# A pooling mixer whose last 32 tokens use a quarter of TensorE's columns, with the norm moved into the pooling matrices

## The chip, the cores and the metric

The kernel runs on one core of one Trainium2 chip. TensorE multiplies matrices and writes to eight banks of PSUM; VectorE (DVE) and ScalarE (ACT) do elementwise work and read those banks; GpSimd (POOL) does a few elementwise operations on SBUF; SyncE (SP) issues nearly all DMAs. The metric is the time of one execution in microseconds of device time. Three runs of the kernel before took 953.94, 954.66 and 955.35 us; their median is 954.66 us.

## What is computed

A decoder of two layers on 256 tokens with 16 meta tokens ahead of them (272 in all), 1024 features wide, in float32. Each layer is a feed-forward network, a mixer and a second feed-forward network, each with an RMS norm before and after it and a residual. The mixer of the first layer averages over the last 2, 4, 8 or 16 tokens, by group of 256 features, and then multiplies each group by its own matrix:

```python
def rmsnorm(x, g):
    y = xf * lax.rsqrt(jnp.mean(xf * xf, axis=-1, keepdims=True) + EPS)
    return (y * g.astype(jnp.float32)).astype(x.dtype)

def causal_multiscale_pool(h, w, b, scale):
    ...
    for g, win in enumerate(POOL_WINDOWS):          # 2, 4, 8, 16
        lo = jnp.maximum(t + 1 - win, 0)
        cnt = (t + 1 - lo).astype(jnp.float32)
        pooled.append((csg[:, 1:, g] - csg[:, lo, g]) / cnt[None, :, None])
    diff = (pooled - hg).astype(h.dtype)
    y = jnp.einsum('blgc,gcd->blgd', diff, w) + b
    return y.reshape(bsz, L, D) * scale

# in the first layer
    f = swiglu(rmsnorm(h, ffn_norm_pre[i, 0]), ...)
    h = h + 0.5 * rmsnorm(f, ffn_norm_post[i, 0])
    hn = rmsnorm(h, mix_norm_pre[i])
    m = causal_multiscale_pool(hn, pool_w[j], pool_b[j], pool_scale[j])
    h = h + rmsnorm(m, mix_norm_post[i])
```

The norm is a factor for each token, the pooling a matrix between tokens, and the group's weights a matrix between features, so the kernel takes them in another order: weights first, then the norm's factor, then the pooling.

## The kernel before

The hidden state `h` lies transposed in SBUF: eight tiles of 128 features by 272 tokens, the 256 tokens first and the 16 meta tokens behind them. Most of the time goes to the products with the weights of the feed-forward networks and of the attention, which TensorE makes in three products for each weight tile (high by high, low by high, high by low). This change touches none of them. It touches `pool_mix`, the mixer of the first layer, which stands between the first feed-forward network (`ffn(0, ...)`) and the second (`ffn(1, ...)`).

The engines PE, ACT, DVE and SP run in the order in which the code is written; what a tile must wait for is worked out from who reads and writes its buffer. A tile with a tag that an earlier tile had takes over that tile's buffer, and its first write waits for the last reader of the earlier one. Two such tags matter here. The mixer's eight weight tiles `wps` (`wp` in the profile) have the tags `xlo0` to `xlo7`; and `Post.old(j)`, which puts `h[j]` times the gain of the next norm into the tile `a` for the next network (line 430), has the tag `xlo{j}` too.

`pool_mix` goes through these steps; lines are those of the profile.

- Twelve products of constants keep TensorE at work while VectorE is alone (line 269, `WARM0`).
- VectorE finishes the post-norm of the network before and adds it onto `h` (lines 701 to 709), tile 0 and tile 1 alone and then two tiles at a time. ScalarE squares `h` two tiles at a time into `psq` (711).
- TensorE makes the inner products with `wps` (690): for each of the eight tiles of `h` one product of 256 columns for each of three blocks of 128 tokens, which are 0 to 127, 128 to 255 and 144 to 271. The third block serves the 16 meta tokens and the 16 tokens at the end. The results `z` fill six banks.
- VectorE adds the squares to `pacc2` (715 to 718) and TensorE sums them over the features, one column for each block (720). These three products stand ahead of the inner products of tiles 6 and 7 (`LATE`).
- ScalarE and VectorE make the reciprocal root (281, 275 to 277) and copy `z` to SBUF times the norm's factor of each token, `zs` (729 to 734).
- For each of the eight output tiles three products with the pooling matrices `bands` (742, 743, 746), whose columns are 128 + 144 + 32; behind each ScalarE squares the result (453), VectorE adds up the squares (464), and for the tiles in `EARLY` VectorE also writes `bt`, the result times its gain (446).
- A few more constant products (`WARM2`), then the tail: `b` of tiles 1 and 2 (435), `bt` of the tiles in `BESIDE`, the sum of squares over the features in two products (470, 471), its reciprocal root `ny` (281), and for the first three tiles of the next network `x = a + b * ny` (312, 314), with which TensorE starts the second network (522).

The lines that set the buffers and the waits in question:

```python
wps.append(act.tile([P, 256], F32, tag=f"xlo{q}", name="wp"))
a = act.tile([P, L], F32, tag=f"xlo{j}", name="a")
```

Of the kernel before, what the change touches and what calls it, by code (L numbers as in the profile page):

```python
# [9 lines left out]
F32 = mybir.dt.float32  # L10
F32R = mybir.dt.float32r
AF = mybir.ActivationFunctionType
ALU = mybir.AluOpType
# [3 lines left out]
P = 128  # L17
D = 1024
NK = D // P
NMETA = 16  # L20
SEQ = 256
L = NMETA + SEQ
# [33 lines left out]
POOL_SQ = ((0, 2), (2, 4), (4, 6), (6, 8))  # L56
# [12 lines left out]


C_FPRE, C_FPOST, C_MPRE, C_MPOST, C_PB, C_PS, C_SUB, C_META = 0, 32, 64, 80, 96, 104, 112, 113
# [108 lines left out]
def trunk(ctx, tc, ht, w13a, w13b, w2t, w2n, wqkva, wqkv, wo, wp, lamv, mask, band, gpost, out):  # L180
    nc = tc.nc
# [5 lines left out]
    tmp = ctx.enter_context(tc.tile_pool(name="tmp", bufs=2))  # L187
# [4 lines left out]
    bands = early.enter_context(tc.tile_pool(name="bands", bufs=1, side="right")).tile([P, 4, 176], F32, name="bands")  # L192
    wps = []
# [53 lines left out]
    pbs = const.tile([P, NK], F32, name="pbs")  # L247
# [152 lines left out]
    class Post:  # L400
# [273 lines left out]
    def pool_mix(old, ps, post):  # L674

        def bank():
            return ps.tile([P, 512], F32, tag="bank", name="bank")


        tok = ((0, P), (P, 2 * P), (L - P, L))  # L680

        z = [[bank() for _ in tok] for _ in range(2)]
        sums = bank()[:, 0:3]
        idle = bank()
        warm(lambda: idle, ones, WARM0, P)

        def inner(j):
            g = j // 2
            for ti, (t0, t1) in enumerate(tok):
                nc.tensor.matmul(z[g // 2][ti][:, (g % 2) * 256:(g % 2 + 1) * 256],  # L690
                                 lhsT=h[j][:, t0:t1], rhs=wps[j], start=j % 2 == 0, stop=j % 2 == 1)

        with tc.tile_pool(name="poolw", bufs=1, reuse_waits="tile") as pw:
            sq = pw.tile([P, NK, L], F32, name="psq")
            zs = [pw.tile([P, D], F32, name=f"zs{ti}", tag=f"zs{ti}") for ti in range(3)]
            ys = []


            old.begin_refine()
            t = tmp.tile([P, L], F32, tag="rt", name="rt")  # L700
            nc.vector.tensor_tensor(t, btall[:, 0], old.y, ALU.mult)
            old.slope()
            nc.vector.scalar_tensor_tensor(t, old.c, 1.5, t, ALU.add, ALU.mult)
            nc.vector.tensor_tensor(h[0], h[0], t, ALU.add)
            old.finish()
            for lo, hi in POOL_H[1:]:
                t = pw.tile([P, 3, L], F32, tag="pt", name="pt", bufs=2)[:, :hi - lo]
                nc.vector.tensor_tensor(t, btall[:, lo:hi], old.r.unsqueeze(1).to_broadcast([P, hi - lo, L]), ALU.mult)
                nc.vector.tensor_tensor(hall[:, lo:hi], hall[:, lo:hi], t, ALU.add)
            for lo, hi in POOL_SQ:  # L710
                nc.scalar.activation(out=sq[:, lo:hi], in_=hall[:, lo:hi], func=AF.Square)
            for j in range(NK - LATE):
                inner(j)
            acc = pw.tile([P, 2, L], F32, name="pacc2")
# [3 lines left out]
            nc.vector.tensor_tensor(acc[:, 0], acc[:, 0], acc[:, 1], ALU.add)  # L718
            for ti, (t0, t1) in enumerate(tok):
                nc.tensor.matmul(sums[:, ti:ti + 1], lhsT=acc[:, 0, t0:t1], rhs=ones[:, 0:1], start=True, stop=True)  # L720
            for j in range(NK - LATE, NK):
                inner(j)
            for j in range(post.ahead):
                post.old(j)
            r2 = rsqrt(sums, 3, True, "rc", 3)

            def normed(q):
                at = slice(q * 512, (q + 1) * 512)
                nc.scalar.mul(out=zs[0][:, at], in_=z[q][0], mul=r2[:, 0:1])
                nc.vector.tensor_scalar(zs[1][:, at], z[q][1], r2[:, 1:2], None, ALU.mult)  # L730
                if q:
                    nc.vector.tensor_scalar(zs[2][:, at], z[q][2], r2[:, 2:3], None, ALU.mult)
                else:
                    nc.scalar.mul(out=zs[2][:, at], in_=z[q][2], mul=r2[:, 2:3])

            def pooled(j):

                y = bank()
                ys.append(y)
                g = j // 2  # L740
                c = slice(j * P, (j + 1) * P)
                nc.tensor.matmul(y[:, P:SEQ], lhsT=zs[1][:, c], rhs=bands[:, g, 0:P], start=True, stop=True)
                nc.tensor.matmul(y[:, 0:P + NMETA], lhsT=zs[0][:, c], rhs=bands[:, g, 0:P + NMETA],
                                 start=False, stop=True, skip_group_check=True)
                ends = y.rearrange("p (a b) -> p a b", b=SEQ)[:, :, 0:NMETA]
                nc.tensor.matmul(ends, lhsT=zs[2][:, c],
                                 rhs=bands[:, g, P + NMETA:].rearrange("p (a b) -> p a b", b=NMETA),
                                 start=False, stop=True, skip_group_check=True)
                post.squared(j, y[:, :L], vt[:, C_PS + j:C_PS + j + 1], pbs[:, j:j + 1], add=False)
                if j:  # L750
# [8 lines left out]
            normed(0)  # L759
            normed(1)  # L760
            for j in range(NK):
                pooled(j)
                if j == 0:
                    first(0)
                if j in EARLY:
                    scaled(j, True)
            s = bank()
            warm(lambda: s, ones, WARM2, P)
            for j in range(1, post.ahead):
                first(j)  # L770
            for j in BESIDE:
                scaled(j, True)
            post.rms(lambda: s, True)
            for j in range(NK):
                if j not in EARLY + BESIDE:
                    scaled(j)
# [395 lines left out]
    with tc.tile_pool(name="ps", bufs=8, space=PSUM) as ps:  # L1172
        warm(lambda: ps.tile([P, 512], F32, tag="bank", name="bank"), ones, WARM_START, P)
        post = Post(L, half[:, 0:8], C_MPRE, AHEAD[0])
# [7 lines left out]
        old, post = post, Post(L, psg, C_FPRE + 8, AHEAD[1])  # L1182
# [36 lines left out]
def _layout(x, meta_tokens, ffn_norm_pre, ffn_norm_post, ffn_w1, ffn_w3, ffn_w2, mix_norm_pre, mix_norm_post,  # L1219
# [42 lines left out]
    t = np.arange(2 * NMETA)  # L1262
    d = np.concatenate([t[NMETA:], t[:NMETA]])[None, None, :] - t[:NMETA, None, None]
    count = np.minimum(np.concatenate([t[NMETA:], t[:NMETA]]) + 1, win)
    ends = np.zeros((P, 4, 2 * NMETA))
    ends[P - NMETA:] = np.where((d >= 0) & (d < win), 1.0 / count, 0.0) - (d == 0)
# [23 lines left out]
```

## Time and profile before

| | before |
|---|---|
| runs | 953.94, 954.66, 955.35 us |
| profiled execution, its time | 954.47 us |
| its span, first to last instruction | 952.7 us |
| mean granted clock of TensorE | 0.998 |
| TensorE's longest gap inside the span | 1.69 us, ahead of 230.54 |

The span is the time from the first to the last instruction of one profiled execution; some 1.8 us of its time lie around it. In the profile PE is TensorE's products, PEld its weight loads. A row of a timeline gives start and duration in us, engine, line, operation, tile written, tiles read, shapes and a count, and in brackets the idle time ahead of it with what ended that. Rows that follow each other with the same line and tiles are merged into one.

### The profile page before, as it was taken

The page shows a single profiled execution, that of the slowest core. Times are in us where ns is not written, and L with a number is a line of the kernel's source. Part 1 is how long each engine was busy: PE and PEld are TensorE (multiplying, and loading weights), DVE is VectorE, ACT ScalarE, POOL GpSimd, SP SyncE. Part 2 cuts the span into 40 slices and gives each one's busy share as a digit, 9 for nine tenths or more (in the row PEclk, how much of TensorE's full clock was granted, in tenths as well). Part 3 has the DMA queues.
Part 4 walks back from the last instruction along what each step waited for, and adds up shares of the span by engine and source line. Part 5 has one row for each costly group of instructions (what it writes and reads, how often), then busy time and mean ns, then how long its engine had stood idle before and what let it go on. Part 6 is the DMA issues. An engine that isn't in the chain of part 4 may idle for free.

```text
span 952.7 us, 17430 instructions
## 1 busy us (share of the span) xinstructions
PE 940.8 (99%) x6937; PEld 904.5 (95%) x6937; DVE 637.2 (67%) x1094; ACT 501.9 (53%) x863; POOL 14.7 (2%) x22
## 2 busy tenths in 40 slices
PE   9999999999999999999999999999999999999997
PEld 9999999998999999999999999999998998888885
DVE  7955554458975555448955554468876899767774
ACT  7744444435654445545744455446776756445442
POOL 0000000210000000000000000000001000000000
PEclk9999999999999999999999999999999999999999
DMA  9755557630375556551755556532523628655521
GB/s 337 239 204 177 166 155 222 219 119 2 116 267 174 175 159 192 179 195 42 257 194 177 163 167 187 187 106 90 177 89 120 212 90 287 223 188 180 185 89 44
DMA packets 48320, 160.74 MB, mean 169 GB/s; under 512 B 5360, under 2 KB 8944, under 8 KB 48240
## 3 DMA queue, kind: packets, MB, share of 16 engines
q1 hardware_dynamic: 47952, 159.31, 52.2%
q8 instruction: 54, 0.88, 0.4%
q10 hardware_dynamic: 288, 0.33, 0.1%
q14 instruction: 26, 0.21, 0.1%
HBM read 158.57 MB, written 1.05 MB: 168 GB/s over the span
## 4 chain that ended last, share of the span: by engine, by line
PE 94%; DVE 3%; ACT 1%; issue 1%; DMA 0%; DVEq 0%; ACTq 0%
PE bank L257 23%; PE bank L256 23%; PE bank L255 23%; PE bank L522 8%; PE bank L1120 7%; PE bank L1122 4%; DVE wlo L149 1%; PE bank L643 1%; PE bank L655 1%; PE bank L644 1%; DMA raw<-in_w13a 0%; ACT sc L844 0%; PE bank L821 0%; PE bank L812 0%; PE bank L811 0%
## 5 line engine op out<-in xcount | busy, mean ns | idle before, releaser
L149 DVE TENSOR_TENSOR wlo<-raw,whi 128x1024 fp32r<-128x1024 f32 (+1 forms) x296 | 353.5, 1197 | 58.9 <-PE bank L256 28.4
L137 ACT CAST whi<-raw 128x1024 fp32r<-128x1024 f32 (+1 forms) x296 | 299.8, 1029 | 51.4 <-PE bank L257 45.9
L255 PE MATMUL bank<-x,whi 128*128 128x272 f32 (+1 forms) x752 | 217.3, 289 | 0.0
L257 PE MATMUL bank<-x,whi 128*128 128x272 f32 (+1 forms) x752 | 216.8, 288 | 0.0
L256 PE MATMUL bank<-x,wlo 128*128 128x272 f32 (+1 forms) x752 | 215.7, 287 | 0.2 <-DVE wlo L149 0.2
L256 PEld LDWEIGHTS bank<-x,wlo 128*128 128x128 f32 x752 | 141.3, 188 | 0.5 <-DVE wlo L149 0.4
L255 PEld LDWEIGHTS bank<-x,whi 128*128 128x128 f32 x752 | 141.3, 188 | 0.5 <-issue 0.4
L257 PEld LDWEIGHTS bank<-x,whi 128*128 128x128 f32 x752 | 141.6, 188 | 0.0
L256 PE MATMUL bank<-ghi,wlo 128*128 128x272 f32 x484 | 140.0, 289 | 0.0
L255 PE MATMUL bank<-ghi,whi 128*128 128x272 f32 x484 | 140.0, 289 | 0.0
L257 PE MATMUL bank<-glo,whi 128*128 128x272 f32 x484 | 140.0, 289 | 0.0
L573 ACT ACTIVATE ua<-ua 128x272 f32<-128x272 f32 (+1 forms) x88 | 37.1, 429 | 143.0 <-DVE ua L559 143.0
L582 ACT CAST ghi<-ua 128x272 fp32r<-128x272 f32 (+1 forms) x88 | 36.1, 417 | 111.7 <-DVE ua L579 111.7
L255 PEld LDWEIGHTS bank<-ghi,whi 128*128 128x128 f32 x484 | 91.8, 190 | 0.0
L257 PEld LDWEIGHTS bank<-glo,whi 128*128 128x128 f32 x484 | 91.2, 188 | 0.0
L256 PEld LDWEIGHTS bank<-ghi,wlo 128*128 128x128 f32 x484 | 90.9, 188 | 0.0
L257 PE MATMUL bank<-xlo,whi 128*128 128x272 f32 x304 | 87.8, 289 | 0.0
L255 PE MATMUL bank<-xhi,whi 128*128 128x272 f32 x304 | 87.4, 287 | 0.0
L256 PE MATMUL bank<-xhi,wlo 128*128 128x272 f32 x304 | 87.3, 287 | 0.0
L579 DVE TENSOR_TENSOR ua<-bank,ua 128x272 f32<-128x272 f32 (+1 forms) x69 | 29.5, 437 | 71.1 <-PE bank L257 71.1
L1120 PE MATMUL bank<-xp,whi 128*128 128x512 f32 x304 | 76.1, 392 | 0.0
L1120 PEld LDWEIGHTS bank<-xp,whi 128*128 128x128 f32 x304 | 55.5, 188 | 10.5
(232 smaller groups left out, 1376.8 us busy)
## 6 DMA issues: line engine op xcount, KB each, us to landing
raw<-in_w13b SPq DMA_DIRECT2D x152, 512.0 KB, 4.1
raw<-in_w2t SPq DMA_DIRECT2D x48, 448.0 KB, 3.4
raw<-in_w2t SPq DMA_DIRECT2D x24, 512.0 KB, 3.5
raw<-in_w2n SPq DMA_DIRECT2D x22, 512.0 KB, 3.8
raw<-in_w13a SPq DMA_DIRECT2D x18, 512.0 KB, 4.2
raw<-in_wqkv SPq DMA_DIRECT2D x18, 512.0 KB, 4.3
raw<-in_wo SPq DMA_DIRECT2D x8, 512.0 KB, 3.7
raw<-in_wqkva SPq DMA_DIRECT2D x6, 512.0 KB, 4.2
```

Of the source, the lines that this page charges most:

```text
L137: self.nc.scalar.copy(out=hi[:, :n], in_=self.raws[u][:, :n])
L149: self.nc.vector.tensor_tensor(lo[:, :n], raw[:, :n], hi[:, :n].bitcast(F32), ALU.subtract)
L255: nc.tensor.matmul(out_ap, lhsT=a[0], rhs=b[0], start=start, stop=False)
L256: nc.tensor.matmul(out_ap, lhsT=a[1], rhs=b[0], start=False, stop=False)
L257: nc.tensor.matmul(out_ap, lhsT=a[0], rhs=b[1], start=False, stop=stop)
L522: nc.tensor.matmul(us[q][:, :n], lhsT=taken[u][a][:, c * P:(c + 1) * P], rhs=x[:, :n], start=start, stop=stop)
L573: nc.scalar.activation(out=a[:, :self.n], in_=a[:, :self.n], func=AF.Silu)
L579: nc.vector.tensor_tensor(s[:, :n], self.sum(u3), s[:, :n], ALU.mult)
L582: nc.scalar.copy(out=hi, in_=s[:, :n])
L643: nc.tensor.matmul(y[:, :n], lhsT=a[0], rhs=x[0], start=b == 0, stop=False)
L1120: nc.tensor.matmul(u, lhsT=parts[0][:, k * P:(k + 1) * P], rhs=res.pairs[k], start=k == 0, stop=k == NK - 1)
L1122: nc.tensor.matmul(u[:, :n], lhsT=parts[1][:, k * P:(k + 1) * P], rhs=res.x[k][0], start=False, stop=k == NK - 1, skip_group_check=True)
```

## The change

Inside `pool_mix`:

- The third token block is gone from the inner products. The last 32 tokens (the 16 at the end and the 16 meta tokens) get products of their own behind the sums, `inner_ends`: 32 tokens wide, so each result takes 32 rows of one bank `ze`. The two tiles of a feature group share 32 rows, and the four groups lie under each other, each on its own quarter of TensorE's columns. Their sums of squares become four products of 32 rows.
- All inner products of the two whole blocks stand ahead of the sums.
- `z` is copied to SBUF without the norm's factor, three of four copies on ScalarE and one on VectorE. The factor goes into the pooling matrices instead: `sb` is `bands` with each row times the factor of its token, made by VectorE, ScalarE and GpSimd, for the first group alone and then for the other three.
- `Post.old` of tiles 0 and 1 stands on ScalarE between the squares of `h` and the copies; tile 2 follows behind `zse`.
- VectorE adds the post-norm onto `h` two tiles at a time from the start, and makes the products of tiles 4 to 7 ahead of their sums.
- The first two output tiles are multiplied before the first product with the ends. Tile 4 goes from `EARLY` to `BESIDE`, so its `bt` is made in the tail.
- The squares of the last output tile but one are no longer added by VectorE: `Post.rms` takes them as a third product.
- `WARM0` goes from 12 to 14 and `WARM2` from 3 to 1. On the host, `band` holds the matrices of the ends at the rows of each group.

```diff
-LATE = 2
-POOL_H = ((0, 1), (1, 2), (2, 4), (4, 6), (6, 8))
-WARM0 = 12
-WARM2 = 3
-EARLY = (0, 3, 4)
-BESIDE = (1, 2, 5)
+WARM0 = 14
+WARM2 = 1
+EARLY = (0, 3)
+BESIDE = (4, 1, 2, 5)
...
-        def rms(self, bank, eps, refill=0):
+        def rms(self, bank, eps, refill=0, apart=1):
...
-            nc.tensor.matmul(s[:, :n], lhsT=ones, rhs=self.sq[NK - 1][:, :n], start=False, stop=True)
+            for j in range(NK - apart, NK):
+                nc.tensor.matmul(s[:, :n], lhsT=ones, rhs=self.sq[j][:, :n], start=False, stop=j == NK - 1)
...
-        tok = ((0, P), (P, 2 * P), (L - P, L))
+        tok = ((0, P), (P, 2 * P))
         z = [[bank() for _ in tok] for _ in range(2)]
+        ze = bank()
...
+        def inner_ends():
+            for j in (0, 2, 4, 6, 1, 3, 5, 7):
+                g = slice(j // 2 * 32, j // 2 * 32 + 32)
+                nc.tensor.matmul(ze[g, 0:256], lhsT=h[j][:, L - 32:L], rhs=wps[j], start=j % 2 == 0, stop=j % 2 == 1)
...
+            product(2)
+            total(2)
+            product(4)
+            product(6)
+            total(4)
+            total(6)
...
-            for j in range(NK - LATE):
+            for j in range(NK):
                 inner(j)
+            for j in range(2):
+                post.old(j)
+
+            nc.scalar.copy(out=zs[0][:, 0:512], in_=z[0][0])
+            nc.scalar.copy(out=zs[1][:, 0:512], in_=z[0][1])
...
+            for g in range(4):
+                nc.tensor.matmul(sums[g * 32:g * 32 + 32, 2:3], lhsT=acc[:, 0, L - 32:L], rhs=ones[:, 0:1],
+                                 start=True, stop=True)
+            inner_ends()
+            nc.scalar.copy(out=zs[0][:, 512:1024], in_=z[1][0])
+            nc.vector.tensor_copy(zs[1][:, 512:1024], z[1][1])
+            r2 = rsqrt(sums, 3, True, "rc", 3)
...
+            nc.vector.tensor_scalar(sb[:, 0, 176:], bands[:, 0, 0:P], r2[:, 1:2], None, ALU.mult)
+            nc.scalar.mul(out=sb[:, 0, 0:P + NMETA], in_=bands[:, 0, 0:P + NMETA], mul=r2[:, 0:1])
+            nc.gpsimd.tensor_scalar(sb[:, 0, P + NMETA:176], bands[:, 0, P + NMETA:], r2[:, 2:3], None, ALU.mult)
+            nc.scalar.copy(out=zse, in_=ze[:, 0:256])
+            for j in range(2, post.ahead):
+                post.old(j)
+            nc.vector.tensor_scalar(sb[:, rest, 176:], bands[:, rest, 0:P], r2[:, 1:2], None, ALU.mult)
+            nc.vector.tensor_scalar(sb[:, rest, 0:P + NMETA], bands[:, rest, 0:P + NMETA], r2[:, 0:1], None, ALU.mult)
+            nc.gpsimd.tensor_scalar(sb[:, rest, P + NMETA:176], bands[:, rest, P + NMETA:], r2[:, 2:3], None, ALU.mult)
...
-            post.rms(lambda: s, True)
+            post.rms(lambda: s, True, apart=2)
```

What stands in the queues at two places. On TensorE, from the inner products to the second output tile, before (the numbers behind `pacc` and `zs` are those of buffers):

```order
L690 MATMUL bank<-wp,h 128x256 x18
L720 MATMUL bank<-ones,pacc_2635 128x1 x3
L690 MATMUL bank<-wp,h 128x256 x6
L742 MATMUL bank<-bands,zs_2590 128x128
L743 MATMUL bank<-bands,zs_2589 128x144
L746 MATMUL bank<-bands,zs_2591 128x2x16
```

The same place in the changed program, whose line numbers differ:

```order
L688 MATMUL bank<-wp,h 128x256 x16
L740 MATMUL bank<-ones,pacc_2601 128x1 x2
L742 MATMUL bank<-ones,pacc_2601 32x1 x4
L694 MATMUL bank<-wp,h 32x256 x8
L767 MATMUL bank<-sb,zs_2591 128x128
L768 MATMUL bank<-sb,zs_2590 128x144
L767 MATMUL bank<-sb,zs_2591 128x128
L768 MATMUL bank<-sb,zs_2590 128x144
L773 MATMUL bank<-sb,zse 128x2x16 x2
```

The last readers of `wp` 0 to 7 moved behind the sums. On ScalarE, from the squares of `h` to the first square of an output tile, with the engines or DMA queues whose semaphores a row waits for; before:

```order
L711 ACTIVATE psq<-h 128x544 [waits DVE_49] x4
L430 ACTIVATE a<-h 128x272 [waits PE_49,Pool_49] x3
L281 ACTIVATE ny<-bank,eps_c 128x3 [waits PE_49]
L729 ACTIVATE zs_2589<-bank,ny 128x512 [waits DVE_49]
L734 ACTIVATE zs_2591<-bank,ny 128x512
L729 ACTIVATE zs_2589<-bank,ny 128x512 [waits PE_49]
L453 ACTIVATE sq<-bank,pbs,h 128x272 [waits PE_49]
```

And in the changed program:

```order
L727 ACTIVATE psq<-h 128x544 [waits DVE_49] x4
L426 ACTIVATE a<-h 128x272 [waits PE_49,Pool_49] x2
L733 COPY zs_2590<-bank 128x512
L734 COPY zs_2591<-bank 128x512
L745 COPY zs_2590<-bank 128x512
L277 ACTIVATE ny<-bank,eps_c 128x3
L752 ACTIVATE sb<-bands,ny 128x144 [waits DVE_49]
L754 COPY zse<-bank 128x256 [waits PE_49]
L426 ACTIVATE a<-h 128x272 [waits Pool_49]
L449 ACTIVATE sq<-bank,pbs,h 128x272 [waits PE_49]
```

Three copies came in between `a` and `ny`, and neither they nor `ny` wait for TensorE themselves any more.

More of the change, by code (lines that the diff above doesn't have):

```diff
@@ L705, in pool_mix @@
+            nc.vector.tensor_tensor(hall[:, 0:2], hall[:, 0:2], t, ALU.add)
             old.finish()
[L706 to L711, printed above, removed]
@@ L712, in pool_mix, with product, total @@
-            for j in range(NK - LATE):
+            acc = pw.tile([P, 2, L], F32, name="pacc2")
+            more = {}
+            def product(lo):
+                more[lo] = pw.tile([P, 2, L], F32, tag="pt", name="pt", bufs=3)
+                nc.vector.tensor_tensor(more[lo], btall[:, lo:lo + 2], old.r.unsqueeze(1).to_broadcast(each), ALU.mult)
+            def total(lo):
+                nc.vector.tensor_tensor(hall[:, lo:lo + 2], hall[:, lo:lo + 2], more[lo], ALU.add)
+            product(2)
@@ L713, in pool_mix @@
+            total(2)
[3 more added lines that the diff above has]
+            total(6)
+            for lo in (0, 2, 4, 6):
+                nc.scalar.activation(out=sq[:, lo:lo + 2], in_=hall[:, lo:lo + 2], func=AF.Square)
+            for j in range(NK):
                 inner(j)
-            acc = pw.tile([P, 2, L], F32, name="pacc2")
+            for j in range(2):
+                post.old(j)
+            nc.scalar.copy(out=zs[0][:, 0:512], in_=z[0][0])
+            nc.scalar.copy(out=zs[1][:, 0:512], in_=z[0][1])
@@ L720, in pool_mix @@
                 nc.tensor.matmul(sums[:, ti:ti + 1], lhsT=acc[:, 0, t0:t1], rhs=ones[:, 0:1], start=True, stop=True)
-            for j in range(NK - LATE, NK):
-                inner(j)
-            for j in range(post.ahead):
-                post.old(j)
[L725 to L734, printed above, removed]
+            for g in range(4):
[5 more added lines that the diff above has]
+            r2 = rsqrt(sums, 3, True, "rc", 3)
+            zse = pw.tile([P, 256], F32, name="zse")
+            sb = pw.tile([P, 4, 176 + P], F32, name="sb")
+            rest = slice(1, 4)
+            nc.vector.tensor_scalar(sb[:, 0, 176:], bands[:, 0, 0:P], r2[:, 1:2], None, ALU.mult)
[3 more added lines that the diff above has]
+            for j in range(2, post.ahead):
+                post.old(j)
+            nc.vector.tensor_scalar(sb[:, rest, 176:], bands[:, rest, 0:P], r2[:, 1:2], None, ALU.mult)
+            nc.vector.tensor_scalar(sb[:, rest, 0:P + NMETA], bands[:, rest, 0:P + NMETA], r2[:, 0:1], None, ALU.mult)
+            nc.gpsimd.tensor_scalar(sb[:, rest, P + NMETA:176], bands[:, rest, P + NMETA:], r2[:, 2:3], None, ALU.mult)
             def pooled(j):
@@ L1264, in _layout @@
     count = np.minimum(np.concatenate([t[NMETA:], t[:NMETA]]) + 1, win)
+    each = np.where((d >= 0) & (d < win), 1.0 / count, 0.0) - (d == 0)
     ends = np.zeros((P, 4, 2 * NMETA))
-    ends[P - NMETA:] = np.where((d >= 0) & (d < win), 1.0 / count, 0.0) - (d == 0)
+    for g in range(4):
+        ends[g * 32 + NMETA:g * 32 + 32, g] = each[:, g]
     r["band"] = c(np.concatenate([inside, ends], axis=2).astype(np.float32))
```

35 lines of the change are left out of this document (19 added, 16 removed).

## The prediction

> **What bounds the kernel now.** I read the page first, then the chain of work that ended last inside the pooling stage, then each engine's timeline there. The page says that TensorE is the bound almost everywhere:
>
> ```profile
> span 952.7 us, 17430 instructions
> PE 940.8 (99%) x6937; PEld 904.5 (95%) x6937; DVE 637.2 (67%) x1094; ACT 501.9 (53%) x863; POOL 14.7 (2%) x22
> ```
>
> The program's order outside the mixer is the same before and after on every engine, so only the mixer counts: it lies between the last product of the first feed-forward network (205.6 us) and the first product of the second (230.54 us). There TensorE isn't the bound throughout. The chain of waits (start, duration, engine, tile, line):
>
> ```profile
> 214.37 0.74 DVE h L709
> ...
> 217.43 0.45 DVE pacc L718
> 217.88 0.04 issue
> 217.92 0.83 PE bank L720 x6
> 218.75 2.70 PE bank L690 x12
> 221.45 0.22 PE bank L742 x2
> ...
> 226.99 0.58 ACT sq L453
> 227.56 0.48 ACT b L435
> 228.04 0.03 issue
> 228.07 1.50 DVE bt L446 x3
> 229.56 0.36 DVE rt L312
> 229.92 0.02 issue
> 229.95 0.45 DVE x L314
> 230.40 0.14 issue
> 230.54 3.53 PE bank L522 x26
> ```
>
> To see here: VectorE adds the post-norm onto `h` until 215.1 and sums the squares until 217.87. TensorE then takes the three sums, the last twelve passes of the inner products, and from 221.3 the eight pooled tiles. A tail on ScalarE and VectorE ends it. I follow one question through the change: when can the first pooled product start, which is at 221.29 now, and is the 9.25 us from there to 230.54 still the same?
>
> **The change, part by part.** *Wider steps on VectorE.* The timeline of VectorE gives the durations (start, duration, engine, line):
>
> ```profile
> 207.45 0.44 DVE L701 TENSOR_TENSOR rt<-bt,ny 128x272 f32<-128x272 f32 x1 [5.39 <-ACT ny L281]
> 208.14 0.44 DVE L505 SCALAR_TENSOR_TENSOR nt<-bank,nt 128x272 f32<-128x272 f32 x1 [0.25 <-ACT nt L502]
> 211.58 0.72 DVE L709 TENSOR_TENSOR h<-h,pt 128x544 f32<-128x544 f32 x1
> ```
>
> One tile takes 0.44, two take 0.72; a step that needs the one before starts 0.03 after its end, another 0.08 before it. The five one-tile steps for tiles 0 and 1 become three two-tile steps (2.2 to 2.16 us), and with the products of 4 to 7 put ahead of their sums most steps no longer need the one just before them. Laid out one after another, the starts are 207.45, 208.14, 208.62, 209.38, 210.02 and 210.56, then 211.31, 211.95, 212.59, 213.22 and 213.87: `h` is whole at 214.6 instead of 215.1, and the sum of squares at 217.4 instead of 217.87. The first tile comes 0.56 later (210.1), and two more warming products cover that. **Gain 0.5 us so far.**
>
> *Inner products.* The timeline of TensorE:
>
> ```profile
> 217.92 0.83 PE L720 MATMUL bank<-ones,pacc 128*128 128x1 f32 x6
> 218.61 2.84 PE L690 MATMUL bank<-wp,h 128*128 128x256 f32 x12
> ```
>
> A product is two passes (x12 for the order's x6), and a pass of 256 columns takes 2.84 less its last drain of 0.38 over 11, 0.22 us. The 32 passes that stay end with 16 passes that start when `h` 4 and 5 are there (213.95 plus 0.1): 217.5. The sums follow without a wait: four full passes and eight narrow ones. The nearest row with a narrow pair is in the attention stage, where the last two of the six passes have 16 columns:
>
> ```profile
> 649.97 0.63 PE L921 MATMUL bank<-ones,acc 128*128 128x1 f32 x6
> ```
>
> It is no longer than six full ones (0.83), so I give all sums 0.9, and the products into quarter columns start at 218.4. Whether these run beside each other no row shows for columns. From both sides: one after another they take 16 passes of 0.22, 3.5 us; four at once 0.9 us. The nearest rows are products on halves of the array's rows in the attention stage:
>
> ```profile
> 657.33 0.52 PE L811 MATMUL bank<-kf,qf 64*128 64x144 f32 x4
> 657.68 0.63 PE L812 MATMUL bank<-kf,qf 64*128 64x272 f32 x4
> ```
>
> Four passes of 272 columns would need 0.92 at 0.23 each; they take 0.63 with the drain, so two stand beside two. I take 0.9 and keep 3.5. The Trainium skill, TensorEngine Tiling (Array Packing), section Key Properties, says that different tiles run their loads and products in parallel; by that rule it would be 0.9, and the row agrees for halves of the rows.
>
> *The two early `a` tiles on ScalarE.* This decides. `a` of tile 0 and tile 1 has the tag of the buffer that held the mixer's weights `wp` 0 and 1. Its write must wait for the last product that reads them. That was an early inner product; it is now a quarter-column product, behind the sums. The rows of order above show it: the three copies of `z` and the table's `ny` follow on ScalarE with no wait on TensorE of their own, so the wait in front of them covers the sums too. ScalarE takes its instructions in the program's order. Its timeline before:
>
> ```profile
> 215.13 0.66 ACT L711 ACTIVATE psq<-h 128x544 f32<-128x544 f32 x1 [0.74 <-DVE h L709]
> 215.69 1.33 ACT L430 ACTIVATE a<-h 128x272 f32<-128x272 f32 x3
> 218.79 0.26 ACT L281 ACTIVATE ny<-bank,eps_c 128x3 f32<-128x3 f32 x1 [1.76 <-PE bank L720]
> 219.74 0.69 ACT L729 ACTIVATE zs<-bank,ny 128x512 f32<-128x512 f32 x1 [0.69 <-DVE ny L277]
> ```
>
> Now: the last square ends at 215.3, and ScalarE stands still until the first quarter product has drained, at 219.0 (218.4 plus two passes and a drain of 0.16). `a` 0 starts at 219.1. The fifth quarter product, which frees `wp` 1, is done at 219.4 (side by side), `a` 1 at 219.5, 0.41 later (1.33 for three, each 0.51 long). Then three copies of 512 columns out of the bank; the last network has the same shape:
>
> ```profile
> L1140 ACT COPY hn<-bank x4: 576/578/581, 828.8 to 880.1; 128x512 f32<-128x512 f32 x4
> ```
>
> With 0.1 overlapping that is 0.48 each: 219.9, 220.4, 220.9. `ny` runs at 221.35 to 221.6, where it ran at 218.79. What is queued behind the wait is thus everything that the norm needs, and VectorE, GpSimd and TensorE wait for it. Three short steps on VectorE follow:
>
> ```profile
> 219.08 0.16 DVE L275 TENSOR_TENSOR nt<-ny 128x3 f32<-128x3 f32 x1 [1.22 <-ACT ny L281]
> 219.54 0.16 DVE L277 SCALAR_TENSOR_TENSOR ny<-nt,ny 128x3 f32<-128x3 f32 x1
> ```
>
> They took 0.65 from `ny`'s end; the norm is there at 222.3 instead of 219.7. The scaled matrix of 128 columns costs VectorE between those 0.16 and the 0.35 of 256 columns (row below); with the hand-over the first pooled product starts at **222.6, 1.3 us later than now**. That the two big evacuations with the norm are gone (0.69 and 0.75 each) and that a third of the inner products is gone is eaten by the wait.
>
> ```profile
> L419 DVE TENSOR_SCALAR b<-bt,h x4: 349/354/356, 745.7 to 752.0; 128x256 f32<-128x256 f32 x4
> L666 POOL TENSOR_SCALAR wp<-wp,h 128x256 f32<-128x256 f32 x8 | 9.1, 1150 | 184.1 <-DMA wp<-in_wp 178.5 <-PE bank L257 5.6
> ```
>
> The other scalings lie beside TensorE: VectorE's 384 and 432 columns are each under 0.75 (`zs` of 512, from the bank) and done by 223.6, needed at 224.1. GpSimd's 32 and 96 columns lie between 0.1 and 1.15 each; I take 0.2 and 0.5, needed at 223.6 and 224.3. At the upper end of both, TensorE would wait 0.5 more. The copy of `zse` (256 columns) is done by 223.0, needed at 223.6.
>
> *The tail.* The pooled tiles are the same 24 products. Two warming products go (0.45), one more product of squares comes (two passes, 0.46), and VectorE has one sum less and one `bt` more behind the last tile. VectorE's queue (three `bt`, then `rt`) ended only 0.1 after `ny` was ready in the chain above. I cost it at nothing, between -0.2 and +0.2: the 9.25 us stay.
>
> *The clock.* The wait leaves TensorE idle from 219.45 to 222.6, 3.15 us; today's longest gap there is 1.69. What a gap does to the granted clock shows at the kernel's end (windows: length, busy by engine with PE first, granted clock, DMA) and at its start, where as many passes of one line were counted in two equal windows:
>
> ```profile
> 942.00:946.00 4.00, 4.00 (x19) 3.05 (x17) 3.10 (x9) 1.67 (x5) 0.00 (x0) 1.00 0.09 34
> 946.10:948.70 2.60, 0.00 (x0) 0.00 (x0) 1.83 (x6) 0.98 (x3) 0.00 (x0) 1.00 0.39 135
> 948.80:951.40 2.60, 0.00 (x0) 0.00 (x0) 0.82 (x3) 0.00 (x0) 0.00 (x0) 0.50 0.56 202
> 5.30:6.60 1.30, 1.30 (x7) 1.30 (x7) 1.00 1.00 340
> 6.70:8.00 1.30, 1.30 (x13) 1.30 (x12) 1.00 0.91 213
> ```
>
> After 2.6 to 2.7 us without a product the clock was at half. At the start passes came half as fast until between 6.6 and 6.7 us, 5.7 us after the first product at 0.97. A gap of 1.69 us left it whole. At 3.15 us I expect half a clock from somewhere in the gap on. Bounds: nothing, and 5.7 us at half rate, which is 2.8 us lost. I take the middle, **1.5 us**. The Trainium skill, TensorE: Matmul & The Clock Gate, section What's actually happening, gives an idle window of about 3.4 us before the clock falls; by that rule a gap of 3.15 us can't hold a whole window, and the second rival below would come out. The trace's 2.7 us speaks against it.
>
> **Sum.** The profiled execution took 954.47 us (its span of 952.7 and 1.8 around it), 0.19 under the median of three runs, 954.66. Waiting 1.3 plus clock 1.5 gives 957.3 on it and **957.5 us** on the median, 0.3% slower. About 0.2% (1.9 us) is what a measurement of this kernel can tell from no change.
>
> **Rivals.**
> 1. *The columns don't run beside each other.* Then `a` 1 waits for a fifth product that ends at 220.7, the first pooled product is at 223.9, and the gap shrinks to 1.9 us, so the clock mostly stays: 2.6 in all, 957.3; with a halved clock 958.8. Against it: L811 and L812.
> 2. *The clock stays whole* (the other side, not slower by 0.2%). Only the 1.3 remain: 956.0, 0.14%. It decides at the length of gap that halves the clock: over 3.15 us this comes, under it the forecast. For it: one gap is short, and its place against the clock's windows differs by run. Against it: 2.7 us did it at the end.
> 3. *The change does what it is laid out for: ScalarE isn't held* (faster). If the wait in front of `a` were over before 217.5, the copies would run beside the inner products, `ny` at 218.5, the norm at 219.4 and the first pooled product at 219.75: 1.5 less, 953.1. Against it: the shared buffer and the missing waits behind it.
>
> **Chances.** Forecast 0.45, rival 1 0.17, rival 2 0.25, rival 3 0.08, 0.05 for something else. Slower by over 0.2%: forecast, nearly all of rival 1, a tenth of rival 2 and half the rest, 0.66. Faster by over 0.2%: 0.05 (a part of rival 3 and the rest). Within: 0.29. The range of 955.6 to 959.3 takes in the forecast, rival 1 with the halved clock and rival 2 less 0.4, and leaves out rival 3 and the rest.
>
> **What would show it.** ScalarE's idle time before the first `a` ends at a product into quarter columns, near 219; `ny` of three columns starts near 221.4; the first product with `sb` near 222.6; `h` is whole near 214.6. Eight quarter-column products start within 1 us. The granted clock in the windows behind 221 is under 1. Wrong would be: no idle time on ScalarE between the squares and `a`, `ny` before 219.5, or a whole clock throughout.

## The result and the profile after

| | kernel before | changed kernel |
|---|---|---|
| time, median of five runs | 953.96 us | 959.56 us |
| lowest and highest | 953.94 and 955.35 | 957.40 and 961.94 |
| profiled execution, its time | 954.47 | 961.94 |
| its span | 952.7 | 960.1 |

The ratio is 1.0053, with an interval of 1.0033 to 1.0072 (the two medians alone give 1.0059): slower, as forecast, but by 0.53% where 0.30% was forecast. The median lies 0.3 us above the top of the range (959.3). Ratios here and below leave out two stray executions: one of 5267 us in the first experiment and one of 1716 us of the kernel before.

The profiled execution is the slowest of the five, so its extra 7.4 us of span have to be taken apart first. The windows of the changed kernel (start and end, length, then busy time and instructions of TensorE, its weight loads, VectorE, ScalarE and GpSimd, then the granted clock, the DMA share and GB/s) show the clock at the kernel's start and in the mixer:

```profile
8.50:9.80 1.30, 1.30 (x8) 1.30 (x8) 1.30 (x4) 1.13 (x4) 0.00 (x0) 1.00 1.01 314
10.00:11.30 1.30, 1.30 (x12) 1.30 (x12) 1.07 (x3) 1.30 (x3) 0.00 (x0) 1.00 0.99 346
220.80:224.00 3.20, 0.00 (x0) 0.00 (x0) 0.81 (x5) 2.51 (x8) 0.11 (x1) 1.00 0.00 0
225.00:230.00 5.00, 5.00 (x26) 5.00 (x24) 1.85 (x5) 2.67 (x5) 0.01 (x1) 0.50 0.00 0
230.00:235.10 5.10, 5.10 (x23) 4.98 (x24) 1.76 (x5) 2.62 (x5) 0.00 (x0) 0.50 0.00 0
235.20:238.00 2.80, 1.21 (x6) 0.66 (x5) 2.50 (x6) 2.09 (x6) 0.00 (x0) 1.00 0.00 0
```

At the start the passes go from 8 to 12 in 1.30 us: the clock becomes whole at 9.90 us, where the kernel before had that step at 6.66. Half rate thus lasts 3.24 us longer, and half of that, 1.62 us, is the shift of everything behind it: the sums of squares that end the first feed-forward network start at 207.08, before at 205.46. Up to there the two programs are the same, and in the ten experiments below the step lies anywhere from 4.36 to 7.17 us, so it isn't put down to the change; times of the changed kernel are compared below after taking 1.62 off. The recorded clock falls again at 224.94 and is whole at 235.18: 10.24 us at half, three times 3.41. Every stretch at half inside the profiles of this document is a multiple of 3.41 us, so that length is called a window of the clock. Three rows of TensorE in the kernel before, for comparison:

```profile
205.46 0.62 PE L470 MATMUL bank<-pacc,ones 128*128 128x272 f32 x2
221.29 0.38 PE L742 MATMUL bank<-bands,zs 128*128 128x128 f32 x2
230.54 1.00 PE L522 MATMUL bank<-x,whi 128*128 128x272 f32 x6 [1.69 <-DVE x L314]
```

ScalarE's timeline in the mixer of the changed kernel, and TensorE's:

```profile
215.61 1.29 ACT L727 ACTIVATE psq<-h 128x544 f32<-128x544 f32 x2 [1.25 <-DVE h L718]
220.42 0.95 ACT L426 ACTIVATE a<-h 128x272 f32<-128x272 f32 x2 [3.52 <-PE bank L694]
221.28 0.56 ACT L733 COPY zs<-bank 128x512 f32<-128x512 f32 x1
222.69 0.28 ACT L277 ACTIVATE ny<-bank,eps_c 128x3 f32<-128x3 f32 x1
```

```profile
219.64 0.24 PE L742 MATMUL bank<-ones,pacc 128*32 128x1 f32 x8
219.72 1.05 PE L694 MATMUL bank<-wp,h 128*32 128x256 f32 x16
224.10 0.46 PE L767 MATMUL bank<-sb,zs 128*128 128x128 f32 x2 [3.33 <-ACT sb L752]
229.99 0.78 PE L767 MATMUL bank<-sb,zs 128*128 128x128 f32 x2
238.03 0.99 PE L520 MATMUL bank<-x,whi 128*128 128x272 f32 x6 [1.62 <-DVE x L310]
```

To see here: ScalarE stands still for 3.52 us in front of the first `a` and is released by a quarter-column product. Its copies and the norm's table are queued behind it, and TensorE then stands still for 3.33 us. The first pooled product starts at 222.48 (224.10 less 1.62), 1.19 later than in the kernel before. From there to the next network it is 13.93 us (238.03 less 224.10), before 9.25: 4.68 more, with one tile's products taking 1.33 us where they took 0.69. The parts add up: 1.62 of the start, 1.19 of waiting, 4.68 in the tail, less 0.07 behind it, 7.4.

### The profile page after: what moved, and what is told of

It is laid out like the page before. It is cut to its first block, busy times and chain, and to the rows that moved or that the text cites. A ratio compares the mean times of both kernels' runs of the same rounds, so it can differ in the third digit from the quotient of the medians.

```text
span 960.1 us, 17454 instructions
## 1 busy us (share of the span) xinstructions
PE 944.6 (98%) x6945; PEld 908.3 (95%) x6945; DVE 636.5 (66%) x1092; ACT 502.4 (52%) x865; POOL 15.3 (2%) x24
## 3 DMA queue, kind: packets, MB, share of 16 engines
HBM read 158.57 MB, written 1.05 MB: 166 GB/s over the span
## 4 chain that ended last, share of the span: by engine, by line
PE 95%; DVE 2%; ACT 1%; issue 1%; DMA 0%; DVEq 0%; ACTq 0%
PE bank L253 23%; PE bank L252 23%; PE bank L251 22%; PE bank L520 8%; PE bank L1150 7%; PE bank L1152 4%; PE bank L688 1%; DVE wlo L145 1%; PE bank L641 1%; PE bank L653 1%; PE bank L642 1%; PE bank L767 0%; DMA raw<-in_w13a 0%; ACT sc L874 0%; PE bank L265 0%
## 5 line engine op out<-in xcount | busy, mean ns | idle before, releaser
L251 PE MATMUL bank<-x,whi 128*128 128x272 f32 (+1 forms) x752 | 217.4, 289 | 0.0
```

The costliest lines, as they stand in the source:

```text
L251: nc.tensor.matmul(out_ap, lhsT=a[0], rhs=b[0], start=start, stop=False)
```

## The experiments

The main theory: `a` 0 and `a` 1 share buffers with the mixer's weights 0 and 1, so ScalarE waits for quarter-column products, which delays the norm by about 1.2 us; the gap that this leaves on TensorE halves its clock, and that costs the rest. Rivals: the norm is late for another reason; the new products or the tail are slow by themselves. All experiments were timed against runs of the kernel before on the same chip (medians of 954.25, and 954.38 for the last two). The moment at which the clock becomes whole at the start shifts each profile a little; times "in the time of the kernel before" are taken from the start of the last sums of the first network.

**Warming products in the gap.**

```diff
             inner_ends()
+            warm(lambda: idle, ones, 12, P)
             nc.scalar.copy(out=zs[0][:, 512:1024], in_=z[1][0])
```

> The changed kernel with twelve warming products (24 passes of 128 columns, 2.7 us) behind the quarter-column products, in the gap that TensorE has there. If the gap halves the clock and the halved clock carries most of the loss: the granted clock stays whole through the mixer, the gap shrinks from 3.3 to about 0.6 us, the first pooled product starts where it started (the norm is as late as before), the stretch from there to the next network is about 9.3 us again instead of 13.9, and the time is 1.2 us over the kernel before: 955.2. Rival: the new products themselves (pooling matrices scaled, narrow ends) are slower or the tail on ScalarE is; then the stretch stays near 13 us and the time near 959.

Measured: 955.58, ratio 1.0012 (1.0003 to 1.0021). Its TensorE timeline at the end of the gap, and the window from the first pooled product to the end of the mixer:

```profile
219.13 2.94 PE L265 MATMUL bank<-ones 128*128 128x128 f32 x24
222.53 0.46 PE L768 MATMUL bank<-sb,zs 128*128 128x128 f32 x2 [0.46 <-ACT sb L753]
```

```profile
222.53:231.90 9.37, 7.63 (x56) 6.88 (x57) 6.80 (x16) 7.83 (x17) 0.91 (x2) 1.00 0.01 2
```

The norm is as late as in the changed kernel (222.48 in the time of the kernel before), the clock is whole, and the stretch is 9.38 instead of 13.93. So of the 5.3 us between the changed kernel's median and that of the kernel before in these runs, 4.0 (959.56 less 955.58) are the halved clock and 1.3 (955.58 less 954.25) are the wait. (The changed kernel's own median was taken in other runs, against 953.96 for the kernel before, so the 4.0 is good to some tenths.) The new products and the tail aren't slow by themselves.

**The two `a` tiles issued later.**

```diff
-            for j in range(2):
-                post.old(j)
             nc.scalar.copy(out=zs[0][:, 0:512], in_=z[0][0])
...
-            for j in range(2, post.ahead):
+            for j in range(post.ahead):
                 post.old(j)
```

> The changed kernel with the first two a tiles issued behind the copy of zse, where the third is. If ScalarE's wait for the shared buffer is what delays the norm: no idle time in front of the first copy of z beyond 217.5 (in the time of the kernel before), ny of three columns at about 218.5 instead of 221.1, first pooled product at about 219.8, no gap over 1 us, clock whole; the three a tiles (1.33 us) now lie in front of the first square on ScalarE and give back 0.5 to 1.0: 953.2, 0.1% under the kernel before. Rival: the norm is late for another reason (the copies out of the banks, the hand-over to VectorE); then the first pooled product stays near 222.5 and the time near 959.

Measured: 952.77, ratio 0.9986 (0.9977 to 0.9995). The first pooled product starts at 219.13, 219.72 in the time of the kernel before, with a gap of 0.57, and the stretch behind it takes 9.39. The three `a` tiles in front of the first square cost nothing that shows: that square starts 1.39 behind the first pooled product, and 1.35 in the next experiment, where two of the three lie elsewhere.

**The same order, other buffers for the weights.**

```diff
-wps.append(act.tile([P, 256], F32, tag=f"xlo{q}", name="wp"))
+wps.append(act.tile([P, 256], F32, tag=f"xlo{q}" if q > 1 else f"xhi{q + 6}", name="wp"))
```

> The changed kernel in its own order, but the mixer weights 0 and 1 lie in the dead buffers of x tiles 6 and 7, so that a 0 and a 1 share nothing with them. If the shared buffer is the cause: both a tiles start right behind the last square, near 215.7 in the time of the kernel before, the copies at about 217.5, ny of three columns at 218.5, first pooled product near 219.8, no gap of TensorE over 1 us, clock whole, nothing given back behind it: 952.5, 0.15% under the kernel before. Rival (the order on ScalarE matters and not the buffer): as the changed kernel, near 959.

Measured: 952.70, ratio 0.9983 (0.9974 to 0.9992). Its ScalarE and TensorE timelines:

```profile
214.63 0.92 ACT L426 ACTIVATE a<-h 128x272 f32<-128x272 f32 x2
215.46 0.56 ACT L733 COPY zs<-bank 128x512 f32<-128x512 f32 x1
217.77 0.26 ACT L277 ACTIVATE ny<-bank,eps_c 128x3 f32<-128x3 f32 x1 [0.39 <-PE bank L742]
```

```profile
219.16 0.46 PE L767 MATMUL bank<-sb,zs 128*128 128x128 f32 x2 [0.56 <-ACT sb L752]
228.53 0.99 PE L520 MATMUL bank<-x,whi 128*128 128x272 f32 x6 [1.62 <-DVE x L310]
```

To see here: with the order on ScalarE unchanged, no idle time stands in front of `a`, `ny` follows its sums after 0.39, and the first pooled product is at 219.72 in the time of the kernel before, 1.57 earlier than there. The shared buffer was the cause, and without it the change gains 1.6 us: this version beats both kernels.

**Quarter-column products ahead of the sums.**

```diff
+            inner_ends()
             for ti, (t0, t1) in enumerate(tok):
                 nc.tensor.matmul(sums[:, ti:ti + 1], ...)
...
-            inner_ends()
```

> The changed kernel with the quarter-column products ahead of the three sums. The first of them then ends about 0.7 us earlier, so a 0, the copies and ny too: first pooled product near 221.8 in the time of the kernel before, a gap of TensorE of 2.3 to 2.6 us. If a gap has to be longer than that to halve the clock: 954.5. If 2.6 us is enough: up to 958, with runs that differ by some microseconds. Rival (the hold isn't the cause of the late norm): first pooled product near 222.5, as in the changed kernel.

Measured: 958.36 (957.14 to 959.19), ratio 1.0040 (1.0027 to 1.0053). The first pooled product is at 222.09 in the time of the kernel before, 0.39 earlier than in the changed kernel (0.7 was expected): the quarter-column products themselves start only 0.42 earlier, at 217.68 against 218.10, because the inner products stand in front of them. The gap of 2.63 us halved the clock in the profile, and the mean granted clock of all five runs is 0.993 to 0.995 (the kernel before: 0.997 to 0.999). The windows around the fall:

```profile
217.00:218.80 1.80, 1.80 (x29) 1.10 (x28) 0.69 (x1) 1.01 (x3) 0.00 (x0) 1.00 0.00 0
218.90:220.20 1.30, 0.00 (x0) 0.00 (x0) 0.00 (x0) 1.30 (x4) 0.00 (x0) 1.00 0.00 0
220.30:221.40 1.10, 0.00 (x0) 0.00 (x0) 0.84 (x5) 0.41 (x3) 0.14 (x1) 0.50 0.00 0
```

The clock fell at 220.28, when TensorE had stood still for only 1.43 us. In front of that, in the same window, ran quarter-column products and 0.8 us of sums with one column: TensorE was busy, but the sums stream hardly anything. So the length of the gap alone doesn't decide, which led to the two experiments with thin products.

**A gap in the kernel before, with nothing else of the change.**

```diff
+            late = pw.tile([P, 2, L], F32, name="late")
+            for _ in range(9):
+                nc.scalar.activation(out=late, in_=hall[:, 0:2], func=AF.Square)
             r2 = rsqrt(sums, 3, True, "rc", 3)
```

> The kernel before, with nine squares of two tiles (0.63 us each, the result isn't used) put on ScalarE ahead of the norm's table, so that TensorE gets a gap of about 3 us ahead of the first pooled tile, and nothing else of the change. The wait itself is 3.2 us: 957.4. If the halved clock behind such a gap costs what it cost in the changed kernel (about 4, from that kernel with and without warming products): 961.4. If it costs the 1.5 of the prediction: 958.9. If the changed products (scaled matrices, narrow ends) were what kept the clock low, and not the gap: 957.4 to 958.9.

Measured: 961.08 (957.64 to 961.88), ratio 1.0060 (1.0046 to 1.0075). The gap became 3.34 us and the wait 3.5, so 957.8 without any loss of clock. One run did take 957.64, with a mean clock of 0.999; the others took 959.05 to 961.88 at 0.993 to 0.996. Windows of the profiled one:

```profile
221.70:224.90 3.20, 0.00 (x0) 0.00 (x0) 1.30 (x5) 2.44 (x6) 0.00 (x0) 1.00 0.00 0
225.70:232.40 6.70, 6.70 (x33) 6.70 (x32) 3.29 (x8) 3.56 (x7) 0.00 (x0) 0.50 0.00 0
232.50:235.90 3.40, 3.13 (x23) 2.62 (x22) 1.99 (x5) 2.90 (x6) 0.00 (x0) 1.00 0.00 0
```

The gap alone can halve the clock, and cost up to 4 us, with the pooled products as they were; the changed products aren't needed for it.

**A shorter gap.** Six warming products instead of the twelve above.

> The changed kernel with six warming products instead of twelve in the gap (12 passes, 1.4 us), so that TensorE stands still for 1.9 us. The gap of 1.6 to 1.7 at the end of the mixer left the clock whole, one of 2.6 us halved it in each of five runs. If the length of the gap within a window decides: whole in most runs, 955.6, with single runs above 957. If any gap near 2 us is enough: 958 to 959.

Measured: 955.82, ratio 1.0019 (1.0009 to 1.0028). Eight of eleven runs took 955.37 to 956.03 at a mean clock of 0.998 or 0.999, three took 958.6 at 0.995. The profile is of one of the three; its gap was 1.80 us:

```profile
220.60:222.20 1.60, 0.00 (x0) 0.02 (x1) 0.91 (x5) 0.91 (x4) 0.21 (x1) 1.00 0.00 0
222.30:223.90 1.60, 1.60 (x15) 1.60 (x16) 0.58 (x2) 0.91 (x3) 0.82 (x2) 1.00 0.00 0
224.00:227.30 3.30, 3.30 (x18) 3.30 (x16) 1.91 (x5) 2.12 (x5) 0.00 (x0) 0.50 0.02 5
```

The clock fell at 223.97, 1.8 us after TensorE had begun to work again: the window of 3.41 us that had just ended, of which about half was idle (1.66 us), was looked back on. This profile has a second such stretch, 234.21 to 237.62, behind the gap of 1.91 us at the end of the mixer, so its 3 us are those of two windows at half. Where a gap lies against the windows differs from run to run, and so gaps near 2 us sometimes cost something and mostly nothing.

**Dense products behind the gap.**

```diff
+            for _ in range(16):
+                nc.tensor.matmul(idle[:, 0:P + NMETA], lhsT=ones[:, 0:P], rhs=sb[:, 0, 0:P + NMETA], start=True, stop=True)
             pooled(0)
```

> The changed kernel with its gap kept, and between the gap and the first pooled tile sixteen products of ones with the first scaled matrix (32 passes of 144 columns each close behind another; 4.3 us at full clock, 8.6 at half), whose result isn't used. Asked: what keeps the clock at half for three windows of 3.41 us in the changed kernel. Theory D, the pooled tiles' products are too thin (short passes with gaps between them): with dense products the clock is whole again after the first window that lies within them, so at most 6.8 us behind the start of the products, and the record shows one or two windows at half. Theory F, three windows are fixed once the clock has fallen: 10.24 us at half as in the changed kernel. The time is 959.6 plus 4 to 6 by D, plus 8 or more by F.

Measured: 960.75, ratio 1.0069 (1.0057 to 1.0081). Its windows, from the end of the gap on:

```profile
222.50:223.50 1.00, 1.00 (x8) 1.00 (x9) 0.61 (x2) 0.61 (x2) 0.85 (x2) 1.00 0.00 0
223.60:226.90 3.30, 3.30 (x16) 3.30 (x15) 0.00 (x0) 0.00 (x0) 0.00 (x0) 0.50 0.00 0
227.00:230.40 3.40, 3.40 (x31) 3.40 (x31) 0.00 (x0) 0.95 (x3) 0.00 (x0) 1.00 0.02 5
```

One window at half (223.57 to 226.98), against three in the changed kernel: three are not fixed. The times in the expectation were added up wrongly for both theories: with the clock whole again ahead of the pooled tiles, their 4 us aren't lost, so the base is 955.6 and not 959.6. The added products took 5.69 us, which gives 961.3.

**Thin products behind the gap, and with no gap.** The same addition in the changed kernel, and in the version with other buffers, with forty products of 32 columns:

```diff
+            for _ in range(40):
+                nc.tensor.matmul(idle[:, 0:32], lhsT=ones[:, 0:P], rhs=sb[:, 0, 0:32], start=True, stop=True)
             pooled(0)
```

> The changed kernel with its gap kept, and between the gap and the first pooled tile forty products of 32 columns (80 passes, whose result isn't used). A pass of 32 columns follows the last after 0.115 us at full clock (0.53 for four against 0.30 for two), as one of 128 columns does, so TensorE is busy all the time but streams a quarter of the columns. Theory D (thin products don't raise the clock): at half until the end of them, 18 us and more, and into the pooled tiles: 955.6 plus 18.4 plus 0 to 4, 974 to 978. Theory F (three windows, whatever runs): 10.24 us at half, 955.6 plus 14.4: 970. A busy TensorE raises it as dense products did: one or two windows at half, 966 to 968.

> The kernel with weights 0 and 1 in other buffers (952.7, no gap over 0.6 us in front of the pooled tiles), with the same forty thin products in front of the first pooled tile. If only standing still lowers the clock: whole throughout, 80 passes of 0.115 more: 961.9. If what counts is how much TensorE streams in a window: the clock falls 3.4 to 6.8 us behind the start of the products, though TensorE doesn't stand still, the passes after it take twice as long and the pooled tiles start at half: 965 to 971.

Measured: 975.11 (973.50 to 976.62) with the gap and 969.15 (967.26 to 972.21) without. The windows of the first, and TensorE's row and the windows of the second:

```profile
223.90:237.90 14.00, 14.00 (x67) 14.00 (x68) 0.00 (x0) 0.00 (x0) 0.00 (x0) 0.50 0.00 1
238.00:244.20 6.20, 6.20 (x29) 6.20 (x30) 1.42 (x4) 2.67 (x5) 0.00 (x0) 0.50 0.00 0
244.30:248.30 4.00, 4.00 (x30) 3.49 (x28) 2.58 (x7) 3.25 (x6) 0.00 (x0) 1.00 0.00 0
```

```profile
219.43 14.04 PE L787 MATMUL bank<-sb,ones 128*128 128x32 f32 x80 [0.60 <-ACT sb L752]
```

```profile
219.50:222.90 3.40, 3.40 (x31) 3.40 (x32) 0.56 (x2) 0.56 (x2) 0.80 (x2) 1.00 0.00 0
223.10:233.20 10.10, 10.10 (x49) 10.10 (x48) 0.00 (x0) 0.00 (x0) 0.00 (x0) 0.50 0.01 2
```

Both times lie where the expectations have them if thin products don't raise the clock and if too little streamed lowers it (974 to 978, and 965 to 971). With the gap the clock stayed at half for 20.48 us, six windows, while TensorE was busy without a break; a seventh, from 251.11, came behind the gap of 1.91 us at the end of the mixer. Without a gap it fell at 223.02, 3.6 us into the thin products, with TensorE not idle at all in the window of 3.41 us ahead of that. What decides is how much is streamed in a window, not whether TensorE is busy; how much is counted further down.

**The old tail behind the new head.** In the version with other buffers, `apart=1`, three warming products and the kernel before's `EARLY` and `BESIDE`.

> The changed kernel with weights 0 and 1 in other buffers (952.7), and behind the pooled tiles the kernel before's order: seven sums of squares on VectorE and one on TensorE, three warming products, three early and three late scalings on VectorE. The prediction costed that part of the change at nothing, within 0.2. The stretch from the first pooled product to the next network is 9.25 in the kernel before and 9.39 here with the new order: 952.6 if the old order is the shorter by those 0.14, 952.7 if the pooled products' own order makes the difference.

Measured: 953.09, ratio 0.9988 (0.9980 to 0.9997). The stretch from the first pooled product is 9.73, not 9.25: TensorE's timeline shows its first sum waiting for VectorE.

```profile
226.29 0.73 PE L467 MATMUL bank<-pacc,ones 128*128 128x272 f32 x2 [0.49 <-DVE pacc L460]
229.10 1.25 PE L520 MATMUL bank<-x,whi 128*128 128x272 f32 x6 [1.62 <-DVE x L310]
```

The expectation was wrong: the new tail is 0.36 shorter than the old one behind this head. Three of its eleven runs took 954.4 to 954.6 at a mean clock of 0.997; the profile is of one, and there the clock fell to half for one window behind the gap of 1.62 at the mixer's end.

## Why the prediction was right in kind and wrong in size

Times of the changed kernel here are less 1.62.

- *Wider steps on VectorE*: held. `h` is whole at 214.59 (214.6 forecast), the sum of squares at 217.36 (217.4).
- *Inner products*: held, a little quicker. The quarter-column products start at 218.10 (218.4), because the sums held them up for 0.5 us and not 0.9. Their 16 passes of 256 columns took 1.05 us with the last drain. One after another they would take 3.5, so four stand beside each other on the array, and the first rival, which had them in a row, is out.
- *The wait on ScalarE*: held, step by step. Release at 218.80 (219.1), `ny` at 221.07 (221.35), first pooled product at 222.48 (222.6): 1.2 later than before, where 1.3 was forecast. Two experiments that take this wait away by different means, by order and by buffer, both bring the first pooled product to 219.72 (the third rival had 219.75) and the time to 952.8 and 952.7 (it had 953.1). The third rival was right about the gain and wrong about the program: ScalarE was held.
- *The tail*: held. 9.38 at whole clock against 9.25, within the 0.2. That its new order is worth 0.36 behind the earlier head was not seen.
- *The clock*: right in kind, and the term of the sum that failed in size. "Bounds: nothing, and 5.7 us at half rate, which is 2.8 us lost. I take the middle" cost 1.5; it measured 4.0 between the medians and 4.55 between the profiled tails (13.93 and 9.38), above the upper bound. The 5.7 us came from the kernel's start, where wide products run one behind another. The pooled tiles behind the gap stream less, and the clock stayed at half for 10.24 us; it fell only 0.84 us behind the end of the gap (224.94 against 224.10), so none of that time was spent idle in the gap, where the prediction let it begin. The step took how long the clock stays low for a property of the clock, where it depends on what TensorE is given to do at that moment.
- *The clock stays whole* (second rival): its price was right, its condition not met. 956.0 was forecast, and 955.58 is what the kernel takes with the gap filled. Without filling, none of the five runs was below 957.4.

The sum on the medians: 1.3 of waiting and 4.0 of clock, 5.3, where 1.3 and 1.5 were forecast.

The Trainium skill, TensorE: Matmul & The Clock Gate, section What's actually happening, has the clock fall after at least one idle window of about 3.4 us and rise after a busy one. The length of the window agrees: every stretch at half inside these profiles is one, two, three, four or six times 3.41 us. The two conditions don't, if idle and busy are read as the profile counts them. Here the clock fell after windows with 1.4 to 1.9 us of standing still, and with thin products and no gap after one with none at all, and stayed low through several windows in which TensorE was busy all the time. The measurement decides.

A count over the twelve profiles shows what stands in place of idle and busy. For each window of 3.41 us it adds up how long the columns streamed in it take at whole clock: 0.86 ns a column in the mixer (256 in 0.22 us), 0.46 ns in the networks (272 in 0.125 us), and a quarter of that for products on a quarter of the array's columns. It is an estimate, with windows laid at the recorded steps of the clock. From the start of the kernel to 940 us, every window with less than 1.23 us was followed by half clock and every one with more than 1.40 us by whole clock, whichever clock it had itself; in between both occur. The window that ends at the fall of the clock had 0.76 us in the changed kernel; forty thin products left 0.83 a window at whole clock and 0.44 at half, the dense ones 1.77 at half. The pooled tiles at half clock come to 1.26, 1.27 and 1.43 in the changed kernel, and to 1.32 and 1.34 in the kernel before with its gap: they lie at the bound, so it takes them three windows or two. The late start of the changed kernel's profile fits too: the window up to 6.48 us has 1.32 at half clock, and the next was at half again.

The same count separates two windows that were idle for the same 1.69 us at the end of the mixer: 1.48 us streamed in the kernel before, whole afterwards, and 1.40 in the version with the old tail, half afterwards. Gaps of 1.91 us there left the clock whole in two profiles and halved it in two. Open is where between 1.23 and 1.40 us the bound lies. Open too is how many windows each run of the changed kernel spent at half, since only one was traced; the mean clocks of the five, 0.993 to 0.997, say that it was not the same number.

## What to carry to other kernels

Before an instruction is moved ahead in an engine's order, look at whose buffer it writes: a shared tag turns an early step into a wait for the last reader, and everything behind it in that engine's queue pays. A gap on TensorE is priced by what runs behind it, at half clock, until enough is streamed in one window again; short passes can make that several windows. If a gap can't be closed, products that nobody reads are a cheap cover: twelve of them won back 4.0 us here, though closing the gap was worth 2.9 us more (955.58 and 952.70).

## What the runs showed of the hardware

A pass of 32 columns costs TensorE as much time as one of 128 (31 passes in 3.40 us, 0.11 each, where 24 warming passes of 128 columns took 2.94 with the drain; both load weights for every pass), and yet doesn't keep its clock up: eighty of them without a gap took 14.04 us instead of 8.8 (80 times 0.11). The clock goes by what is streamed in windows of 3.41 us: under 1.23 us of it in one, counted at whole clock, the next was at half; over 1.40, whole. And the moment at which the clock becomes whole at the start, 4.36 to 9.90 us in twelve profiles, moved the profiled execution of the changed kernel by 1.62 us, almost a third of what the change cost.
